# Two directions of an RWKV-7 scan: the chunk inverse multiplied onto the score rows outside the chain, 64-row score tiles, and a plain float32 output product

## The chip, the cores and the metric

The kernel runs on one core of one Trainium2 chip. The metric is the device time of one execution in microseconds (us), given as the median of several runs. PE is TensorE, DVE is VectorE, ACT is ScalarE, POOL is GpSimd, SP is SyncE, which here issues most of the DMAs.

## What is computed

One step of a two-layer trunk on 640 tokens (128 of a prompt, 512 of a sample) of 1024 features. Layer 0 mixes tokens with a spatial gate, layer 1 with RWKV-7, once forward and once backward in time; each is followed by an MLP. The change lies in layer 1. For each of 16 heads of 64 features a 64 x 64 state S is carried from token to token:

```python
def step(s, inp):
    r_t, w_t, k_t, v_t, kk_t, a_t = inp
    sa = jnp.einsum('bhij,bhj->bhi', s, -kk_t)
    s = (s * w_t[:, :, None, :]
         + sa[..., None] * (kk_t * a_t)[:, :, None, :]
         + v_t[..., None] * k_t[:, :, None, :])
    return s, jnp.einsum('bhij,bhj->bhi', s, r_t)
```

The outputs of the two directions are added, normalized per head, given a bonus term, multiplied by a gate, `g = sigmoid(xg @ g1) @ g2`, and go through `w_o` into the residual x.

## The kernel before

**Number format.** Most weight products split weights and activations into two parts of a fast format (float32r, "hi" and "lo") and add three products: hi hi, hi lo, lo hi. In the output product `mm3` does this. Other products are plain float32, which PE runs as two passes; each shows as two records in the trace.

**Tiles.** Features lie on partitions, 8 tiles of 128 features, two heads each (64 rows each). Tokens are cut into 10 chunks of 64 for each head, 2 of the prompt and 8 of the sample. q numbers pairs of chunks, e the chunk in a pair, ti one of the two feature tiles that are worked on together, d the direction, h the head in a tile. A group g is two feature tiles in one direction; there are 8 groups.

**Projections** (`rwkv_project`, lines 462 to 808). Tile t goes through the products for r, the low-rank decay and rate products (lines 624 to 626, PSUM tag z with two buffers), a quarter of the v products, and `finish` with `prep` for both directions (lines 629 to 669). `prep` makes running products of decays in Pt, then KR (k^ and r times decays, lines 651 and 653) and IT (the two kinds of state update rows, lines 660 to 665), and stores both to DRAM. KR, IT, Pt have one buffer each, tw two. For tiles 0 and 1 `score` (line 671) also makes the products IT^T k^ that a chunk's inverse takes and copies them to AT; the later tiles' come from the scans' fronts. The last tile's `finish` runs during the first scans.

**Inverse.** Within a chunk the tokens depend on each other; this is solved with a triangular 64 x 64 inverse for each chunk and head: 32 x 32 blocks by substitution on POOL and DVE (`inv_sub`), then two rounds of 32 x 32 products on PE (`merges`, gps and tps) that give TT, for a whole group at a time.

**Fronts** (`Front`, lines 884 to 933). A unit is one chunk pair of one feature tile, ten per group. `load` brings W (k^ and r rows of both heads with zeros in the other head's half, so that a 128-row product can serve both; the zeros are written to DRAM once, line 1608) and IT. `p1` multiplies them (p, line 910, two products of 256 columns), `ev` masks the scores into W and B and copies those that the inverse takes to AT, `tr` transposes IT (line 932) into B.

**The chain** (`part1`, `part2`). It runs through the chunks of a group. RZ holds, for each chunk, the state in one half of the partitions and v (later the solved rows) in the other. In a step, for each of the two feature tiles: za = W^T RZ (line 1026), a copy to zs on ACT (1029), za = TT^T zs (1039), two evacuations on ACT into RZ (1042). Meanwhile sy takes the state (1034, with an identity) and the r rows (1036); then come the products with B (1053, 1054), two evacuations on DVE with the decay factor into the next chunk's RZ (1060), and Y's (1063, 1065). The prompt's 2 chunks and the sample's 8 are independent, so that in a group's first four steps the two alternate.

**Order.** The code issues everything in program order, with hand-made tables that say at which of 20 positions of a group (two per step) a front's parts, the inverse, the merges, the adaLN products (`ada_core`) and the output product come. The chain's instructions have a higher priority, so a scheduler moves them ahead of others. Each engine then runs its own list in order.

**Output product** (`Tail`). `gate` multiplies y by the gate product; `early` does the first four feature tiles of w_o in groups 6 and 7, `end` the other four after the last step; weights and activations are split on ACT and on DVE or POOL (lines 1226 and 1227, 1192 and 1193).

## Time and profile before

| what | us |
|---|---|
| runs: median of 3 (lowest, highest) | 2092.6 (2089.22, 2100.25) |
| profiled execution: first to last instruction (span; the page gives no other time of it) | 2109.0 |
| PE busy in it | 1991.5 |
| DVE busy | 1162.9 |
| ACT busy | 774.5 |
| POOL busy | 389.3 |
| projections, last two thirds | 850 to 1072 |
| scans, from the first product with B to the last | 1107 to 1593 |
| after the scans, until layer 1's MLP | 1593 to 1636 |

The profile is one execution of its own, and its span is 16.4 us above the median of the runs. A row of the trace's groups reads: line, engine, operation, output tile from input tiles, form, count, then busy us and mean ns of one, then the idle time of the engine ahead of it and what ended it. A product's form "128*64" is rows by columns of the array that it takes; "128x64" is its moving operand. The record of a product spans its way through the array too, so the distance between two starts tells what one costs, and the sum of lengths does not. The granted clock is the share of full speed that TensorE's throttle passed.

### The profile page before, as it was taken

The numbers are of one execution on the slowest core, as the hardware profiler recorded it, in microseconds if no ns is written. First come the engines' busy times: TensorE is split into PE (matmuls) and PEld (weight loads), VectorE is DVE, ScalarE is ACT, GpSimd is POOL, SyncE is SP. The second block draws the span as 40 slices with busy tenths as digits, with TensorE's granted clock in tenths as the row PEclk, the third lists the DMA queues.
The fourth block names the chain that finished last, engine by engine and source line by source line (L and its number), as shares of the span: only waits on it lengthen the run. The fifth ranks groups of instructions, "written<-read, shape, count | busy, mean of one in ns | idle before, by whom it ended". The sixth has DMA issues, their size and how long they took to land.

```text
span 2109.0 us, 39157 instructions
## 1 busy us (share of the span) xinstructions
PE 1991.5 (94%) x15882; PEld 1739.6 (82%) x15882; DVE 1162.9 (55%) x2308; ACT 774.5 (37%) x1737; POOL 389.3 (18%) x689
## 2 busy tenths in 40 slices
PE   6999999999999789988869999999998999999997
PEld 5777889999999678877747766767787999999996
DVE  5435643333333796766786577787658533333334
ACT  5323531312222255444524444554434522222231
POOL 0000000000000200477551465465201000000000
PEclk9999999999999889987869879998799999999998
DMA  8777352222222033554655444552242222222221
GB/s 286 265 266 233 105 184 80 71 81 70 80 71 75 36 96 121 171 151 129 186 159 175 143 131 148 166 160 80 71 130 76 67 74 75 76 74 77 73 67 51
DMA packets 124438, 254.58 MB, mean 121 GB/s; under 512 B 24417, under 2 KB 63969, under 8 KB 124129
## 3 DMA queue, kind: packets, MB, share of 16 engines
q1 hardware_dynamic: 123824, 251.62, 37.3%
q8 instruction: 125, 2.05, 0.4%
q14 instruction: 57, 0.46, 0.1%
q10 hardware_dynamic: 432, 0.46, 0.1%
HBM read 214.67 MB, written 45.22 MB: 123 GB/s over the span
## 4 chain that ended last, share of the span: by engine, by line
PE 85%; DVE 6%; POOL 3%; ACT 2%; issue 2%; DMA 1%; SPq 0%; DVEq 0%; POOLq 0%; ACTq 0%
PE fmps L114 47%; PE zps L310 6%; PE p L910 4%; PE wops L1180 3%; PE vps L751 2%; PE za L1039 2%; PE za L1026 2%; PE sy L1053 2%; PE sy L1034 1%; PE rps L114 1%; PE trps L932 1%; PE adaps L1166 1%; PE adaps L122 1%; PE sy L1036 1%; PE tps L980 1%
## 5 line engine op out<-in xcount | busy, mean ns | idle before, releaser
L114 PE MATMUL fmps<-ahi,whi 128*128 128x256 f32 (+1 forms) x2272 | 534.6, 310 | 4.9 <-ACT ahi L100 3.1
L114 PE MATMUL fmps<-alo,whi 128*128 128x256 f32 (+1 forms) x2272 | 533.8, 309 | 1.3 <-DVE alo L101 1.3
L114 PE MATMUL fmps<-ahi,wlo 128*128 128x256 f32 (+1 forms) x2272 | 533.8, 309 | 0.0
L114 PEld LDWEIGHTS fmps<-ahi,whi 128*128 128x128 f32 x2272 | 414.4, 188 | 11.0 <-ACT ahi L100 6.3
L114 PEld LDWEIGHTS fmps<-alo,whi 128*128 128x128 f32 x2272 | 415.0, 188 | 2.1 <-DVE alo L101 1.8
L114 PEld LDWEIGHTS fmps<-ahi,wlo 128*128 128x128 f32 x2272 | 415.2, 188 | 1.0 <-issue 0.8
L88 ACT CAST whi<-wraw 128x1024 fp32r<-128x1024 f32 x174 | 182.6, 1050 | 632.6 <-PE fmps L114 538.2
L89 DVE TENSOR_TENSOR wlo<-wraw,whi 128x1024 fp32r<-128x1024 f32 x174 | 214.4, 1233 | 276.2 <-ACT whi L88 276.1
L283 DVE SCALAR_TENSOR_TENSOR x<-fmps,mod,x 128x128 f32<-128x128 f32 (+2 forms) x153 | 74.5, 527 | 305.4 <-PE fmps L114 305.4
L491 POOL TENSOR_TENSOR xx<-h 128x254 f32<-128x254 f32 (+1 forms) x16 | 12.1, 754 | 721.2 <-DVE h L210 706.1
L841 POOL TENSOR_TENSOR inv<-inv 128x220 f32<-128x220 f32 (+29 forms) x217 | 100.7, 464 | 114.4 <-DVE inv L834 57.7
L910 PE MATMUL p<-W,IT 128*128 128x256 f32 x320 | 109.6, 453 | 10.0 <-DVE B L925 5.9
L843 POOL TENSOR_TENSOR inv<-inv 128x220 f32<-128x220 f32 (+29 forms) x217 | 104.5, 482 | 16.9
L1042 ACT ACTIVATE RZ<-za 64x64 f32<-64x64 f32 x320 | 58.4, 214 | 66.7 <-PE za L1039 53.9
L1060 DVE TENSOR_TENSOR RZ<-sy,PC 64x64 f32<-64x64 f32 x256 | 49.4, 219 | 60.2 <-PE sy L1054 52.5
L101 DVE TENSOR_TENSOR alo<-rsq,ahi 128x640 fp32r<-128x640 f32 (+2 forms) x69 | 53.6, 776 | 45.6 <-ACT ahi L100 45.3
L100 ACT CAST ahi<-rsq 128x640 fp32r<-128x640 f32 (+2 forms) x69 | 47.5, 689 | 82.2 <-DVE rsq L435 81.8
L910 PEld LDWEIGHTS p<-W,IT 128*128 128x128 f32 x320 | 57.9, 211 | 22.9 <-DVE B L925 6.3
L1054 PE MATMUL sy<-RZ,B 128*64 128x64 f32 x640 | 72.6, 251 | 0.6 <-ACT RZ L1042 0.6
L1026 PEld LDWEIGHTS za<-RZ,W 128*64 128x64 f32 x640 | 43.5, 154 | 33.8 <-DVE RZ L1060 9.0
L1026 PE MATMUL za<-RZ,W 128*64 128x64 f32 x640 | 62.5, 254 | 8.4 <-DVE RZ L1080 5.9
L1036 PE MATMUL sy<-RZ,W 128*64 128x64 f32 x640 | 69.1, 249 | 0.0
(289 smaller groups left out, 3428.4 us busy)
## 6 DMA issues: line engine op xcount, KB each, us to landing
wraw<-w SPq DMA_DIRECT2D x126, 512.0 KB, 3.5
wraw<-ada SPq DMA_DIRECT2D x64, 512.0 KB, 4.9
W<-dKR SPq DMA_DIRECT2D x80, 256.0 KB, 3.5
adaw<-adac SPq DMA_DIRECT2D x32, 512.0 KB, 4.4
dKR<-zero SPq DMA_DIRECT2D x32, 320.0 KB, 6.3
dKR<-KR SPq DMA_DIRECT2D x32, 320.0 KB, 4.1
dIT<-IT SPq DMA_DIRECT2D x16, 640.0 KB, 3.3
IT<-dIT SPq DMA_DIRECT2D x80, 128.0 KB, 2.9
```

What stands on the lines that cost most here:

```text
L88: act.copy(hi[:, :n], r[:, :n])
L89: vec.tensor_tensor(out=lo[:, :n], in0=r[:, :n], in1=hi[:, :n], op=ALU.subtract)
L114: pe.matmul(ps[:, PS0 + t0:PS0 + t1], w, x[:, t0:t1], start=start, stop=stop)
L283: vec.scalar_tensor_tensor(out=X[n][:, t0:t1], in0=ps[:, t0 - r[0]:t1 - r[0]], scalar=mod[l][:, which, n, g:g + 1], in1=X[n][:, t0:t1], op ...
L310: pe.matmul(pss[i], x[:, i * P:(i + 1) * P], w[:, kq * 512:(kq + 1) * 512], start=(k == 0 and j == 0), stop=(k == KT - 1 and j == 2))
L841: eng.tensor_tensor(out=tv, in0=LA[:, s + 1:32, s:s + 1].to_broadcast([P, n, m]), in1=LX[:, s:s + 1, c0:c1].to_broadcast([P, n, m]), op=AL ...
L843: eng.tensor_tensor(out=LX[:, s + 1:32, c0:c1], in0=LX[:, s + 1:32, c0:c1], in1=tv, op=ALU.subtract)
L910: pe.matmul(ps[:, :, 2 * e:2 * e + 2].rearrange("p h s t -> p h (s t)"), IT[:, e], W[:, :, 2 * e:2 * e + 2].rearrange("p h s t -> p h (s t ...
L1026: pe.matmul(za[a0:a0 + 64, 0], W[:, h, 3 * e], RZ[:, ti, h, c], start=True, stop=True)
L1036: pe.matmul(sy[y0:y0 + 64, h], W[:, h, 1 + e], RZ[:, ti, h, c], start=h == 0, stop=False)
L1054: pe.matmul(sy[y0:y0 + 64, h], B[:, h, 3 * e], RZ[:, ti, h, c], start=False, stop=h == 1)
L1180: pe.matmul(ps, u, v, start=start and j == 0, stop=stop and j == 2)
```

## The change

1. **Chain.** New `wt` and `wp` make, per unit and before the chain gets there, WP: the k^ rows, an identity block and the masked scores, multiplied by the inverse TT. In the chain one product with WP (za) stands in place of two with a copy between. Its evacuation goes to ACT for one head and DVE for the other, and so does that of the next state. za has one PSUM buffer for both feature tiles instead of two.
2. **64-row tiles.** `load` brings T (k^ and IT, 128 rows, no zero halves) and the r rows into buffers whose other halves were zeroed once. `p1` makes eight products per unit on 64 rows, four with r and four with an identity (which replaces the transposes); the halves of the two heads go to different PSUM banks. p's PSUM tag has one buffer of two banks, shared with `wp`; `wt` has one bank, q. The 32 stores of zeros are gone.
3. **Scores in the projections.** `score` now runs for all tiles; from tile 2 on the result goes through tw to DRAM, and `load_AT` brings it back for a group.
4. **Output product.** Plain float32 instead of `mm3`: no splits, one product (two records) instead of three.
5. **Tables.** Merges come earlier in a group, fronts ahead of them are spread over the group, adaLN products start in group 2 instead of 3.

```diff
-                nc.sync.dma_start(out=dr["IT"][d, t], in_=IT.rearrange("p c s t -> p (c s t)"))
-                if t < 2:
-                    score(t, d, KR, IT)
+                nc.sync.dma_start(out=dr["T"][d, t, :, :, 2:6], in_=IT.rearrange("p (q e) s t -> p q (e s) t", e=2))
+                score(t, d, KR, IT, tw)
...
-                    u = U0[d] + 10 * t + 5 * b
-                    act.copy(ATs[d][:, u:u + 5], ps)
+                    if t < 2:
+                        u = U0[d] + 10 * t + 5 * b
+                        act.copy(ATs[d][:, u:u + 5], ps)
+                    else:
+                        act.copy(tw[:, 5 * b:5 * b + 5], ps)
+                if t >= 2:
+                    nc.sync.dma_start(out=dr["AT"][d, t], in_=tw)
...
-            cp = Pool(es, "cc", {"W": NL, "B": NL, "I": 5, "TT": 2})
+            cp = Pool(es, "cc", {"T": 6, "B": 8, "WT": 3, "WP": 8, "R": NR, "TT": 2, "b": 14})
...
-            pf = Pool(es, "cpf", {"p": 2, "m": 1}, PSUM)
+            pf = Pool(es, "cpf", {"p": 1, "q": 1, "m": 1}, PSUM)
...
+            Rs = [cp.tile([P, 2, 2, 64], F32, "R", f"R{j}") for j in range(NR)]
+            for R in Rs:
+                vec.memset(R, 0.0)
...
                 def p1(self, i):
                     u = self.buf[self.units[i]]
-                    W, B, IT, _ = u
-                    ps = pf.tile([P, 2, 4, 64], F32, "p", "p1")
+                    R, Tt = u[0], u[3]
+                    B = cp.tile([P, 2, 4, 64], F32, "B", "B")
+                    ps = pf.tile([P, 2, 8, 64], F32, "p", "p1")
                     for e in range(2):
-                        pe.matmul(ps[:, :, 2 * e:2 * e + 2].rearrange("p h s t -> p h (s t)"), IT[:, e],
-                                  W[:, :, 2 * e:2 * e + 2].rearrange("p h s t -> p h (s t)"), start=True, stop=True)
-                    u[3] = ps
+                        for h in range(2):
+                            a0 = 64 * h
+                            it = Tt[a0:a0 + 64, 2 + 2 * e:4 + 2 * e].rearrange("p s t -> p (s t)")
+                            pe.matmul(ps[:, h, 3 * e], it, R[a0:a0 + 64, h, e], start=True, stop=True)
+                        for h in range(2):
+                            a0 = 64 * h
+                            it = Tt[a0:a0 + 64, 2 + 2 * e:4 + 2 * e].rearrange("p s t -> p (s t)")
+                            pe.matmul(ps[:, h, 1 + e], it, ident[a0:a0 + 64, a0:a0 + 64], start=True, stop=True)
+                    vec.tensor_tensor(out=B[:, :, 0:4:3], in0=ps[:, :, 0:4:3], op=ALU.mult,
+                                      in1=masks[:, self.d, 1].unsqueeze(1).unsqueeze(1).to_broadcast([P, 2, 2, 64]))
+                    act.copy(B[:, :, 1:3], ps[:, :, 1:3])
+                    u[1] = B
...
+                def wt(self, i):
+                    u = self.buf[self.units[i]]
+                    Tt = u[3]
+                    ps = pf.tile([P, 2, 2, 64], F32, "q", "wtps")
+                    for e in range(2):
+                        for j in range(2):
+                            for h in range(2):
+                                a0 = 64 * h
+                                x = ident[a0:a0 + 64, a0:a0 + 64] if j == h else Tt[a0:a0 + 64, 3 - h + 2 * e]
+                                pe.matmul(ps[a0:a0 + 64, e, j], Tt[a0:a0 + 64, e], x, start=True, stop=True)
+                    W = cp.tile([P, 2, 2, 64], F32, "WT", "WT")
+                    vec.tensor_tensor(out=W, in0=ps, in1=mT[:, self.d].unsqueeze(1).to_broadcast([P, 2, 2, 64]), op=ALU.mult)
+                    u[3] = W
...
+                def wp(self, i):
                     ti, q = self.units[i]
...
+                    ps = pf.tile([P, 2, 8, 64], F32, "p", "wpps")
                     for e in range(2):
...
+                        for h in range(2):
+                            a0 = 64 * h
+                            pe.matmul(ps[:, h, e], W[a0:a0 + 64, e].rearrange("p s t -> p (s t)"),
+                                      TTs[self.d][a0:a0 + 64, 10 * ti + 2 * q + e], start=True, stop=True)
+                    WP = cp.tile([P, 2, 2, 64], F32, "WP", "WP")
+                    act.copy(WP, ps[:, :, 0:2])
+                    u[2] = WP
...
-                    za = pp.tile([P, 8, 64], F32, f"za{ti}", "za")[:, 0:2]
+                    R, _, WP, _ = fr.buf[ti, q]
+                    za = pp.tile([P, 8, 64], F32, "za", "za")[:, 0]
...
-                        pe.matmul(za[a0:a0 + 64, 0], W[:, h, 3 * e], RZ[:, ti, h, c], start=True, stop=True)
-                    zturn[0] = (zturn[0] + 1) % 4
-                    zs = L0[:, 1536 + 64 * zturn[0]:1600 + 64 * zturn[0]]
-                    act.copy(zs, za[:, 0])
+                        pe.matmul(za[a0:a0 + 64], WP[:, h, e], RZ[:, ti, h, c], start=True, stop=True)
...
-                        pe.matmul(za[a0:a0 + 64, 1], TT[a0:a0 + 64, 10 * ti + c], zs[a0:a0 + 64], start=True, stop=True)
-                    for h in range(2):
-                        a0 = 64 * h
-                        act.activation(out=RZ[a0:a0 + 64, ti, h, c], in_=za[a0:a0 + 64, 1], func=AF.Copy, scale=-1.0)
...
+                    act.activation(out=RZ[0:64, ti, 0, c], in_=za[0:64], func=AF.Copy, scale=-1.0)
+                    vec.tensor_scalar(out=RZ[64:128, ti, 1, c], in0=za[64:128], scalar1=-1.0, scalar2=None, op0=ALU.mult)
...
-                            vec.tensor_tensor(out=dst, in0=sy[s0:s0 + 64, h], in1=pc.to_broadcast([64, 64]), op=ALU.mult)
+                            if h:
+                                act.activation(out=dst, in_=sy[s0:s0 + 64, h], func=AF.Copy, scale=pc)
+                            else:
+                                vec.tensor_scalar(out=dst, in0=sy[s0:s0 + 64, h], scalar1=pc, scalar2=None, op0=ALU.mult)
...
-                            mm3(ps, self.w4[n][k - 4], self.ys[k][h], k == 4, k == 7)
+                            pe.matmul(ps, self.w4[n][k - 4], self.ys[k][h], start=k == 4, stop=k == 7)
...
-            MG = (11, 12, 15, 16, 17, 18, 19)
+            FA = (-8, -6, -4, -2, 0, 2, 4, 6, 8, 10)
+            MG = (4, 5, 7, 8, 9, 10, 11)
```

How the order moves, on PE. First a step of the fifth group, before: za and sy are the chain's first products, L1039 the inverse's, p (L910) and trps (L932) a later unit's front.

```order
L1026 MATMUL za<-RZ,W 64x64 x4
L1034 MATMUL sy<-RZ,cst 64x64 x2
L1036 MATMUL sy<-RZ,W 64x64 x2
L1034 MATMUL sy<-RZ,cst 64x64 x2
L1036 MATMUL sy<-RZ,W 64x64 x2
L1039 MATMUL za<-inv_7286,TT_9340 64x64 x4
L932 MATMUL trps<-cst,IT 128x2x64
L910 MATMUL p_13498<-W,IT 128x2x128 x2
L932 MATMUL trps<-cst,IT 128x2x64
L1053 MATMUL sy<-RZ,B 64x64 x2
```

The same step now: p at L927 (with r) and L931 (with an identity), gps (L1000) the merges' products, sy at L1069 and L1071.

```order
L1064 MATMUL za<-RZ,WP 64x64 x2
L1200 MATMUL adaps<-adaw,cs 32x256
L927 MATMUL p_14344<-R_9565,Tt 128x64 x2
L931 MATMUL p_14344<-cst,Tt 128x64 x2
L927 MATMUL p_14344<-R_9565,Tt 128x64 x2
L931 MATMUL p_14344<-cst,Tt 128x64 x2
L1000 MATMUL gps<-inv,AT 32x32 x3
L1069 MATMUL sy<-RZ,cst 64x64
L1000 MATMUL gps<-inv,AT 32x32
L1069 MATMUL sy<-RZ,cst 64x64
L1071 MATMUL sy<-RZ,R_9572 64x64
L1000 MATMUL gps<-inv,AT 32x32
```

The inverse's products are gone from the step, the two feature tiles' za stand apart, and pieces of other tile forms (64*128 for p, 32*32 for the merges) now stand among the chain's.

The second place is on PE too, in the projections: where a tile's bonus products (bops) and the next tile's norm (rbps) stand, before; vps are products of v, rps of r.

```order
L751 MATMUL vps<-wlo,ahi 128x256
L726 MATMUL bops<-rkh,k 128x2 x5
L114 MATMUL rbps<-rnT,AT 128x256
L114 MATMUL rbps<-rnT,AT 128x384
L114 MATMUL rps<-ahi,whi 128x256
L114 MATMUL rps<-ahi,whi 128x384
L114 MATMUL rps<-alo,whi 128x256
```

And now, at the same tile, with the second direction's scores (aps) four products of v later:

```order
L729 MATMUL bops<-rkh,k 128x2 x5
L114 MATMUL rbps<-rnT,AT 128x256
L114 MATMUL rbps<-rnT,AT 128x384
L754 MATMUL vps<-whi,ahi 128x256
L754 MATMUL vps<-whi,alo 128x256
L754 MATMUL vps<-whi,ahi 128x256
L754 MATMUL vps<-whi,alo 128x256
L677 MATMUL aps<-KR,IT 64x64 x20
L624 MATMUL zps<-hw,l2h 128x320
```

Twenty score products now stand between one tile's last v products and the next tile's decay products, and PE takes them in that order.

More of the change, by code (lines that the diff above doesn't have):

```diff
@@ L935, in inv_start, with load_AT @@
+            def load_AT(g):
+                p, d = divmod(g, 2)
+                for ti in range(2):
+                    u = U0[d] + 10 * ti
+                    nc.sync.dma_start(out=ATs[d][:, u:u + 10], in_=dr["AT"][d, 2 * p + ti])
             def inv_start(d):
@@ L1174, in ada_core, with bank, banks @@
                 gamma(1, 1)
-            def mm3(ps, w, x, start, stop):
-                for j, (u, v) in enumerate(((w[0], x[0]), (w[0], x[1]), (w[1], x[0]))):
-                    pe.matmul(ps, u, v, start=start and j == 0, stop=stop and j == 2)
-            def bank(n, tag="p"):
-                return (pf if tag in "pm" else pp).tile([P, 512], F32, tag, "wops")[:, 0:n]
+            def bank(n, tag="ada"):
+                return (pf if tag in "qm" else pp).tile([P, 512], F32, tag, "wops")[:, 0:n]
+            def banks(n):
+                t = pf.tile([P, 2, 512], F32, "p", "wops")
+                return [t[:, i, 0:n] for i in range(2)]
             def gated(n, ps, x, r):
@@ L1219, in tmp, with load @@
                     return t[:, 0:n]
-                def split(self, src, n, keep=None, eng=vec):
-                    r = self.tmp(n)
-                    nc.sync.dma_start(out=r, in_=src)
-                    hi, lo = (buf(c, [P, 512], F32R, "wos")[:, 0:n] for c in keep) if keep else \
-                        (self.tmp(n, "s"), self.tmp(n, "s"))
-                    act.copy(hi, r)
-                    eng.tensor_tensor(out=lo, in0=r, in1=hi, op=ALU.subtract)
-                    return [(hi[:, c:c + P], lo[:, c:c + P]) for c in range(0, n, P)]
+                def load(self, src, n, keep=None):
+                    r = buf(keep) if keep else self.tmp(n, "s")
+                    nc.sync.dma_start(out=r[:, 0:n], in_=src)
+                    return [r[:, c:c + P] for c in range(0, n, P)]
                 def gate(self, k):
@@ L1289, in late @@
                     nn.acc[1] = fw.tile([P, 384], F32, "acc", "acc1")
-                    self.ys += [full(*parts(fw)) for _ in range(2)]
-                    self.ys += [[one("W", LEN[0]), two("W", LEN[1])] for _ in range(2)]
+                    self.ys += [full(fw.tile([P, T], F32, "a", "ys")) for _ in range(4)]
                     self.fin = [self.finish(*q) for q in ((3, 5), (0, 1), (2, 3), (1, 2))]
@@ L1427, in rwkv_core @@
             pairs = [load_pair(0)]
-            for i in range(4):
-                front(fr[0], i)
             run(m)
@@ L1544, in rwkv_core @@
                 if g == 6:
+                    run(ada)
                     tail = Tail()
@@ L1678, in _pack @@
     d["adac"] = f(aw[1, :, :, 1:].transpose(2, 3, 0, 1, 5, 4, 6).reshape(2, 2, KT, P, 1024))
-    d["zero"] = np.zeros((64, 2 * T), np.float32)
     w = pt(i["sgu_w_in"][0])
```

207 lines of the change are left out of this document (76 added, 131 removed).

## The prediction

> **What bounds the kernel now.** I read the page's chain first: PE carries 85% of it, and most of that is products at line 114 that the change leaves alone. What it touches lies between 850 and 1636 us. There I cut the span into stages by where the scan's products begin and end. Columns: stretch, length, busy us of PE, PEld, DVE, ACT, POOL with instruction counts, granted clock, DMA share, GB/s.
>
> ```profile
> 850.00:1072.00 222.00, 194.57 (x1183) 164.97 (x1182) 151.87 (x131) 108.72 (x176) 137.90 (x172) 0.84 0.55 163
> 1072.00:1107.00 35.00, 20.46 (x216) 14.85 (x218) 31.36 (x65) 4.50 (x13) 21.35 (x42) 0.60 0.52 157
> 1107.00:1593.00 486.00, 477.50 (x5838) 349.81 (x5833) 346.97 (x1083) 226.90 (x888) 201.79 (x414) 0.89 0.44 133
> 1593.00:1636.00 43.00, 36.32 (x225) 32.61 (x225) 34.03 (x102) 19.53 (x47) 4.23 (x3) 0.95 0.21 68
> ```
>
> These are the last two thirds of the projections, the set-up of the scans, the scans, and the output product. In the scans PE looks 98% busy, but a product's record includes its pipeline latency, so that figure is no proof that PE is full. I therefore price PE's work by distances between starts. First the counts in the scan stage, grouped by form (records, then busy us and mean ns; a plain float32 product is two records):
>
> ```profile
> L910 PE MATMUL p<-W,IT 128*128 128x256 f32 x290 | 95.6, 437 | 0.0
> L1054 PE MATMUL sy<-RZ,B 128*64 128x64 f32 x640 | 72.6, 251 | 0.6 <-ACT RZ L1042 0.6
> ...
> L1034 PE MATMUL sy<-RZ,cst 128*64 128x64 f32 x568 | 58.1, 243 | 0.8 <-ACT Y L1063 0.7
> L1039 PE MATMUL za<-inv,TT 64*64 64x64 f32 x636 | 57.7, 250 | 1.5 <-ACT inv L1029 1.5
> L932 PE MATMUL trps<-cst,IT 128*128 128x128 f32 x152 | 38.4, 316 | 0.3 <-ACT B L933 0.3
> L1166 PE MATMUL adaps<-adaw,cs 128*32 128x256 f32 x256 | 32.8, 401 | 0.0
> L980 PE MATMUL tps<-inv 32*32 32x32 f32 x572 | 24.9, 229 | 0.1
> L962 PE MATMUL gps<-inv,AT 32*32 32x32 f32 x560 | 22.3, 228 | 2.1 <-ACT B L933 1.0 <-DVE inv L946 0.7 <-ACT TT L987 0.3
> ```
>
> The timeline gives the distances, at full clock (start, length, what):
>
> ```profile
> 859.10 1.38 PE L679 MATMUL aps<-KR,IT 64*64 64x64 f32 x40
> ...
> 866.03 1.17 PE L726 MATMUL bops<-rkh,k 128*128 128x2 f32 x10
> ...
> 1118.07 0.70 PE L910 MATMUL p<-W,IT 128*128 128x256 f32 x2
> ...
> 1122.19 1.13 PE L910 MATMUL p<-W,IT 128*128 128x256 f32 x4
> 1123.16 0.38 PE L932 MATMUL trps<-cst,IT 128*128 128x128 f32 x2
> ...
> 1396.80 0.22 PE L1036 MATMUL sy<-RZ,W 128*64 128x64 f32 x1
> ...
> 1396.85 0.22 PE L1036 MATMUL sy<-RZ,W 128*64 128x64 f32 x1
> ...
> 1396.91 0.22 PE L1036 MATMUL sy<-RZ,W 128*64 128x64 f32 x1
> 1397.06 0.46 PE L1039 MATMUL za<-inv,TT 64*64 64x64 f32 x8
> ...
> 1398.93 0.64 PE L1166 MATMUL adaps<-adaw,cs 128*32 128x256 f32 x8
> ```
>
> Each run of records ends with about 0.22 us of latency. What is left per record: p 0.216 us ((1.13 - 0.70) / 2); bops 0.106 ((1.17 - 0.22) / 9), which is the weight load alone, since it streams two columns; aps 0.030 ((1.38 - 0.22) / 39) on 64*64 tiles, where the two heads go side by side; ada 0.053; a transpose 0.11. The chain's 128*64 products start 0.057 apart on each of two column tiles, so 0.029 a record. And where the tile form changes (128*64 to 64*64) the next start comes after 0.15 instead of 0.057: 0.093 us for a change of form. From the chain of waits come the 32*32 products (1.24 / 40 = 0.031) and the output product (15.68 / 108 = 0.145):
>
> ```profile
> 1239.64 1.24 PE gps L962 x40
> ...
> 1554.85 15.68 PE wops L1180 x108
> ...
> 1592.69 0.63 ACT wos L1226
> ...
> 1593.38 1.52 POOL wos L1227
> 1594.92 2.52 DMA tmp<-wo
> ```
>
> So PE's work in the scans is: the five groups of 128*64 products, L1054 to L1034 in the rows, some 3,050 records x 0.029 = 88 us; p 63; transposes 17; L1039 19; ada 14; 32*32 35; some 226 output products 33; 60 transposes of y 7: 276. In the order of before I count 793 changes of form from the scans' first to last product: 74. Together 350. The stage offers 486 x 0.89 = 432 us of full clock, so PE waits some 82 us. It is near its own limit; the chain's latency accounts for the rest.
>
> **The change part by part. The chain.** A step loses the score copy, the inverse product, and half of two series of four evacuations, since ACT and DVE now take one head each:
>
> ```profile
> L1029 ACT COPY inv<-za 128x64 f32<-128x64 f32 x160 | 29.4, 213 | 63.9 <-PE za L1026 55.3 <-PE sy L1036 6.9
> ...
> 1397.56 0.68 ACT L1042 ACTIVATE RZ<-za 64x64 f32<-64x64 f32 x4 [0.69 <-PE za L1039]
> ...
> 1398.68 0.73 DVE L1060 TENSOR_TENSOR RZ<-sy,PC 64x64 f32<-64x64 f32 x4 [1.73 <-PE sy L1054]
> ```
>
> 0.21 (copy) + 0.22 (product) + two handovers of some 0.05 + 0.34 + 0.36 = 1.2 us a step, 98 us in 80 steps: more than the 82 that PE waits. The gain cannot exceed those waits.
>
> **Fronts.** Gone are 63 + 17 + 19 = 99 us of PE. In the new order, between the same two ends, stand 624 products of p (64*128), 608 of wt (64*64) and 316 of wp (64*128), two records each. wt goes as aps did: 1216 x 0.030 = 36. The others stream 64 columns under a 128-wide load, so the load sets them: 1880 x 0.106 = 200 us one after another, 100 if the two heads' row tiles run side by side. No row shows 64*128 pairs; aps, whose tiles differ in rows too, is the nearest, so I take 100. Net +37 (or +137).
>
> [...]
>
> **Changes of form.** The new order has 1298 in place of 793, because 64*128 and 64*64 pieces and single 32*32 products stand between the chain's: 505 x 0.093 = +47. Its bounds are 0 (every drain falls where PE waits anyway) and 47; I take 47, as PE is hardly idle.
>
> **Output product.** Three fast passes become two slow ones: for 256 columns 2 x 0.216 = 0.43 against 3 x 0.117 (0.145 x 256 / 320), for 384 0.65 against 0.52: +0.21 a pair. 38 pairs in the scans: +8.
>
> PE's work: 350 + 37 + 47 + 8 = 442 us, over the 432 that the stage has. Of the 82 us of waiting I leave 10. At the same clock: 452 / 0.89 = 508 us, **+22**. With no wait left it is 497 (+11), with all of them 589 (+103).
>
> **Projections.** Scores for all tiles: 12 more bursts of 1.38 us, minus the last tile's, which fall into the scans. Behind each stand its two copies on ACT, then a DMA in SP's queue (behind it the next stores and weight loads), and only then the tw buffer is free for the next tile's ACT op; KR stays held till the products have read it. Times at which a tile's r is evacuated:
>
> ```profile
> 859.74 0.68 ACT L686 COPY r<-rps 128x640 f32<-128x640 f32 x1
> 883.86 0.67 ACT L686 COPY r<-rps 128x640 f32<-128x640 f32 x1
> ...
> 951.99 0.67 ACT L686 COPY r<-rps 128x640 f32<-128x640 f32 x1
> 979.64 0.69 ACT L686 COPY r<-rps 128x640 f32<-128x640 f32 x1 [0.75 <-PE rps L114]
> ```
>
> With scores a tile took 24.1 us, without 27.7, so they can hide: 0. If each of the ten is exposed with one burst and as much again of clearing up, 28. I take **+8**, nearer the rows. Below nothing is excluded: work is only added.
>
> **Set-up**: 12 more memsets on DVE, six p, five wt and four wp instead of four fronts, one more product and copy before the first step, in 35 us of which PE uses 20 at clock 0.60: **+3** (-3 to +12). **Tail**: 32 pairs x 0.21 = +7 after the last step, but the splits on ACT and POOL and the wait for their tile's DMA (0.63 + 1.52 + 2.52 = 4.7, rows above) go: **+2** (-4 to +8). The DVE and ACT work of the other splits hides beside PE now; its going gives nothing. **Zeros**: 32 stores leave SP's queue; PE waited little for them: **-2** (-5 to 0).
>
> ```profile
> PEld adaps L122 <- DMA dKR<-zero: 1.5, 4, 0.4
> ```
>
> The fronts' loads fall in bytes (384 to 256 KB a unit) at a DMA share of 0.44: nothing. Sum: 22 + 8 + 3 + 2 - 2 = +33, made against the profiled execution, whose span is 2109.0 us, 16.4 above the median of the runs. I carry the difference to the median: 2092.6 + 33 = 2126.
>
> **The rivals.** *Faster: the drains lie in the waits.* DVE's evacuations at the end of steps:
>
> ```profile
> 1372.64 0.71 DVE L1060 TENSOR_TENSOR RZ<-sy,PC 64x64 f32<-64x64 f32 x4 [0.51 <-PE sy L1054]
> 1376.44 0.71 DVE L1060 TENSOR_TENSOR inv<-sy,PC 64x64 f32<-64x64 f32 x4 [0.22 <-PE sy L1054]
> ...
> 1386.03 0.73 DVE L1060 TENSOR_TENSOR RZ<-sy,PC 64x64 f32<-64x64 f32 x4 [0.55 <-PE sy L1054]
> 1392.36 0.77 DVE L1060 TENSOR_TENSOR RZ<-sy,PC 64x64 f32<-64x64 f32 x4 [0.17 <-PE sy L1054]
> ```
>
> In a group's first steps, where two chains are independent, a step takes 3.8 us; in the later ones, with one chain, 6.3. That speaks for the chain's latency. If drains cost nothing of their own, waiting is 156 us before; less 98 it is 58, and the stage takes (276 + 45 + 58) / 0.89 = 426: -60, in all 2044; halfway between this and my case is no change. It decides once more than half of the drains and nearly all of the 1.2 us count. Against it: the later steps also carry the merges, and starts on PE stand close together in them.
>
> *Slower by far: row tiles one after another.* (452 + 100) / 0.89 = 620: +134, in all 2238. Against it: aps.
>
> *The clock moves.* It was 0.89 with PE 98% busy. Short 64-row products in place of the 256-column p may lower it; at 0.80 the stage takes 565, +79, in all 2183. A denser PE may keep it at 1.0: 452, -34, in all 2070. [...]
>
> That the chain does not get shorter is excluded: the new order has one product between state and evacuation.
>
> **How the numbers follow.** My case has 0.45 (range 2100 to 2160), one after another 0.14, a lower clock 0.07, drains in the waits 0.27, a higher clock 0.07. About 0.5%, 10 us, is what a measurement can tell here. My case gives 0.40 slower and 0.05 same; drains 0.20 faster and 0.07 same; a higher clock 0.06 faster, 0.01 same; the other two slower. Faster 0.26, same 0.13, slower 0.61. Leaving out the outer half of the two extreme rivals, the range is 2045 to 2215.
>
> **What would show it.** Right: the scan stage near 508 us; in it 64*128 starts some 0.053 us a record, a change of form still 0.15; step ends evener, near 6 us; the projection stage within 10 us of 222. Wrong: steps under 5 us in the later half of a group; 64*128 records 0.106 apart; a granted clock far from 0.89 in the scans; r evacuations over 32 us apart.

## The result and the profile after

| | before | after |
|---|---|---|
| median of 4 runs, us (lowest, highest) | 2092.5 (2089.2, 2100.3) | 2488.2 (2486.0, 2491.4) |
| ratio, 95% interval | | 1.187 (1.183 to 1.192) |
| profiled execution, span | 2109.0 | 2484.6 |
| first product with B, last product with B | 1107.2, 1592.8 | 1083.7, 1956.0 |
| scans between the two | 485.6 | 872.4 |
| after them to the end | 516.2 | 528.6 |

The change made the kernel 18.7% slower; 1.6% was predicted. The spans differ by 375.6 us: 23.5 us less up to the first product with B, 386.8 more in the scans, 12.4 more behind them.

The same stages as in the prediction, cut where they now begin and end (stretch, length, busy us of PE, PEld, DVE, ACT, POOL with counts, granted clock, DMA share, GB/s): the projections, the set-up, the scans, the output product, and the rest.

```profile
850.00:1052.00 202.00, 190.89 (x1558) 162.77 (x1557) 138.06 (x123) 113.08 (x188) 138.98 (x162) 0.93 0.60 186
1052.00:1087.00 35.00, 24.52 (x347) 21.34 (x345) 30.47 (x66) 10.09 (x23) 23.16 (x40) 0.58 0.35 101
1087.00:1956.20 869.20, 866.24 (x7774) 656.57 (x7772) 357.86 (x1002) 202.89 (x640) 187.13 (x420) 0.56 0.24 72
1956.20:2012.00 55.80, 48.19 (x187) 30.51 (x186) 34.22 (x108) 16.39 (x39) 1.27 (x1) 1.00 0.13 46
2012.00:2484.00 472.00, 456.87 (x3092) 454.94 (x3092) 185.62 (x273) 130.39 (x186) 0.00 (x0) 0.98 0.23 71
```

The third row carries the whole result: the granted clock in the scans is 0.56, where before it was 0.89. DVE and ACT are busy for about as long as before (358 and 203 us, against 347 and 227) but now in nearly twice the time, so neither became the bound. The page's slices of 62 us, in tenths, show where it happens:

```profile
PE   7999999999979899989999999999999999999997
PEclk9999999999989999855555555565565999999998
```

PE stands at 9 all through the scans; from the slice at 1056 us to the end of the scans PEclk stands near 5. The products that the change brought are now the costliest groups of the scans (count, then busy us and mean ns of one):

```profile
L931 PE MATMUL p<-cst,Tt 64*128 64x64 f32 x616 | 123.6, 405 | 0.0
L927 PE MATMUL p<-R,Tt 64*128 64x64 f32 x616 | 119.8, 414 | 1.2 <-ACT WP L964 1.2
...
L947 PE MATMUL wtps<-cst,Tt 64*64 64x64 f32 x604 | 98.9, 313 | 0.0
L961 PE MATMUL wpps<-TT,WT 64*128 64x64 f32 x624 | 93.9, 412 | 0.9 <-ACT B L934 0.9
```

**How the clock moves.** The trace gives the granted clock as 1.0 or 0.5, and it changes at multiples of 3.41 us. Three such windows of after, around one change:

```profile
1327.60:1331.00 3.40, 3.40 (x64) 2.28 (x59) 1.93 (x7) 2.48 (x8) 0.00 (x0) 1.00 0.27 69
1331.00:1334.40 3.40, 3.40 (x36) 2.72 (x34) 1.55 (x7) 0.78 (x3) 0.00 (x0) 1.00 0.39 130
1334.40:1337.80 3.40, 3.40 (x43) 2.81 (x42) 1.71 (x7) 1.04 (x4) 0.00 (x0) 0.50 0.52 109
```

PE is busy for 3.40 of 3.40 us in each, and still the clock falls behind the second. A record's length includes its latency (in the prediction's rows sy records are 0.22 us long and start 0.05 to 0.06 apart), so the starts have to be looked at too: in the second window no two follow each other by more than 0.20 us. So no idle gap of anything like a window's length made it fall; there are only the short ones at each change of form, of 0.15 to 0.20 us from start to start. What stands in that window (timeline: start, length, what):

```profile
1331.00 0.33 PE L1084 MATMUL sy<-RZ,B 128*64 128x64 f32 x2
1331.26 0.43 PE L931 MATMUL p<-cst,Tt 64*128 64x64 f32 x2
1331.62 0.34 PE L1064 MATMUL za<-RZ,WP 128*64 128x64 f32 x4
1331.80 0.28 PE L1085 MATMUL sy<-RZ,B 128*64 128x64 f32 x2
1332.01 0.43 PE L931 MATMUL p<-cst,Tt 64*128 64x64 f32 x2
1332.37 0.33 PE L1084 MATMUL sy<-RZ,B 128*64 128x64 f32 x2
1332.62 0.43 PE L927 MATMUL p<-R,Tt 64*128 64x64 f32 x2
```

Every product takes half of the array and streams 64 columns, and the form changes after every two to six records. Compare a window of before that was at half clock and behind which the clock rose, at 1191.3 us:

```profile
1187.90:1191.30 3.40, 3.40 (x27) 2.45 (x26) 2.12 (x10) 0.89 (x3) 2.85 (x8) 0.50 0.56 178
1191.30:1194.70 3.40, 3.40 (x56) 2.62 (x52) 3.24 (x9) 1.87 (x9) 2.93 (x7) 1.00 0.68 204
...
1188.31 0.69 PE L932 MATMUL trps<-cst,IT 128*128 128x128 f32 x2
1188.79 1.91 PE L910 MATMUL p<-W,IT 128*128 128x256 f32 x4
1190.63 0.70 PE L1026 MATMUL za<-RZ,W 128*64 128x64 f32 x8
```

I count a window's *array work*: for each record, rows x columns of the array that it takes x columns streamed, with a p record of before (128 x 128 x 256, 0.216 us at full clock) as the unit; 16 of them would fill a full-clock window, and a float32r record counts half, as by the prediction's estimate from the output product's rows it takes 0.117 us for 256 columns. The window of before holds 4 such records of p, 2 transposes at 0.5, and 8 za records at 1/8, with some nine of sy at 1/8: 7.1 of 16, or 0.44. The window of after holds some 34 records at 1/8: 0.26. Counted so in the scans of all fourteen traces of this study (before, after, twelve experiments):

| array work of a window | at full clock: windows, next one at half | at half clock: windows, next one at full |
|---|---|---|
| under 0.25 | 105, 73 | 885, 18 |
| 0.25 to 0.30 | 113, 42 | 323, 26 |
| 0.30 to 0.34 | 121, 11 | 133, 25 |
| 0.34 to 0.38 | 149, 0 | 47, 33 |
| over 0.38 | 886, 0 | 36, 36 |

No window above 0.34 lost the clock, and few below it won it back. The bounds were read off these same windows, and a record that spans the edge of one can be shared out in other ways; counted where it starts, three of 1042 windows above 0.34 lost the clock, the highest at 0.35. Nothing like this shows when only streamed columns are counted: the windows of before and after behind which the clock fell hold from 0.38 to 0.78 by that count.

The measure is a fair account of the falls and a poorer one of the rises: half of them, 69 of 138, come from windows under 0.34. Many of those hold adaLN products, which take 128 rows but only 32 columns of the array. Of the windows under 0.34 at half clock, 31 of 142 with four or more such records rose, and 26 of 1093 with none. So the array's columns seem to count for less than their share. They do count for something: by rows x streamed columns alone, the clock fell behind windows of up to 0.75. No run here changes the array's columns by themselves, so their weight stays open.

The table also holds a trap. At half clock the same program did about half the work in a window, so what kept the clock up here did not bring it back. After's windows hold 0.46 on average at full clock and 0.21 at half, where only 1.4% are over 0.34; before's hold 0.51 and 0.28, where 16% are. Accordingly before loses the clock nine times in its scans and gets it back after 11 us on average; after loses it six times and stays low for 122 us on average, mostly until a run of adaLN or output products lifts it.

### The profile page after: what moved, and what is told of

Read it like the earlier page. It is cut to its first block, busy times and chain, and to the rows that moved or that the text cites. A ratio compares the mean times of both kernels' runs of the same rounds, so it can differ in the third digit from the quotient of the medians.

```text
span 2484.6 us, 43692 instructions
## 1 busy us (share of the span) xinstructions
PE 2390.1 (96%) x18294; PEld 2046.2 (82%) x18294; DVE 1159.3 (47%) x2229; ACT 758.5 (31%) x1505; POOL 376.0 (15%) x681
## 4 chain that ended last, share of the span: by engine, by line
PE 88%; POOL 4%; DVE 3%; ACT 2%; issue 2%; DMA 1%; SPq 0%; POOLq 0%; DVEq 0%; ACTq 0%
PE fmps L114 40%; PE zps L310 5%; PE wtps L947 4%; PE p L927 4%; PE wpps L961 3%; PE p L931 3%; PE sy L1084 3%; PE za L1064 3%; PE adaps L1200 2%; PE sy L1069 2%; PE wops L1279 2%; PE vps L754 2%; PE sy L1071 2%; PE sy L1085 2%; PE wops L1379 1%
## 5 line engine op out<-in xcount | busy, mean ns | idle before, releaser
L931 PE MATMUL p<-cst,Tt 64*128 64x64 f32 x640 | 128.1, 406 | 0.0
L927 PE MATMUL p<-R,Tt 64*128 64x64 f32 x640 | 124.7, 414 | 1.2 <-ACT WP L964 1.2
L1073 DVE TENSOR_SCALAR RZ<-za 64x64 f32<-64x64 f32 x160 | 36.4, 228 | 188.4 <-ACT RZ L1072 92.5
L1072 ACT ACTIVATE RZ<-za 64x64 f32<-64x64 f32 x160 | 34.7, 217 | 290.2 <-PE za L1064 149.5
L927 PEld LDWEIGHTS p<-R,Tt 64*128 64x128 f32 x640 | 94.7, 295 | 24.0 <-issue 6.0
L1085 PE MATMUL sy<-RZ,B 128*64 128x64 f32 x640 | 112.2, 311 | 0.3 <-ACT RZ L1072 0.2
L931 PEld LDWEIGHTS p<-cst,Tt 64*128 64x128 f32 x640 | 103.4, 304 | 7.7
L843 POOL TENSOR_TENSOR inv<-inv 128x220 f32<-128x220 f32 (+29 forms) x217 | 94.3, 435 | 96.4 <-DVE inv L836 57.4
L947 PE MATMUL wtps<-cst,Tt 64*64 64x64 f32 x640 | 103.9, 312 | 1.1 <-DVE WT L949 1.1
L1071 PE MATMUL sy<-RZ,R 128*64 128x64 f32 x640 | 104.6, 312 | 0.0
L1084 PE MATMUL sy<-RZ,B 128*64 128x64 f32 x576 | 103.3, 313 | 0.6 <-ACT RZ L1072 0.4
L845 POOL TENSOR_TENSOR inv<-inv 128x220 f32<-128x220 f32 (+29 forms) x217 | 98.1, 452 | 16.9
```

What stands on the lines that cost most here:

```text
L843: eng.tensor_tensor(out=tv, in0=LA[:, s + 1:32, s:s + 1].to_broadcast([P, n, m]), in1=LX[:, s:s + 1, c0:c1].to_broadcast([P, n, m]), op=AL ...
L845: eng.tensor_tensor(out=LX[:, s + 1:32, c0:c1], in0=LX[:, s + 1:32, c0:c1], in1=tv, op=ALU.subtract)
L927: pe.matmul(ps[:, h, 3 * e], it, R[a0:a0 + 64, h, e], start=True, stop=True)
L931: pe.matmul(ps[:, h, 1 + e], it, ident[a0:a0 + 64, a0:a0 + 64], start=True, stop=True)
L947: pe.matmul(ps[a0:a0 + 64, e, j], Tt[a0:a0 + 64, e], x, start=True, stop=True)
L1071: pe.matmul(sy[y0:y0 + 64, h], R[:, h, e], RZ[:, ti, h, c], start=h == 0, stop=False)
```

## The experiments

The edits are shown shortened. Theory A: the clock follows array work, and the 64-row products with 64 columns each let it fall; what it costs is the time at half clock. Rivals: another part of the change holds it down (B: the chain without its waits, the form changes, the tables), or TensorE is throttled because it no longer idles (C). For each run the row of its scans from the end of the first step to the end of the last is shown. It is of one execution, and small differences of its clock are not safe: before's trace has a granted clock of 0.937 over the whole execution, its other executions in this study mostly 0.934 to 0.951. Length x clock is the time that the scans would take at full clock, if all of it went with the clock; for before and after these rows are

```profile
1111.00:1593.00 482.00, 473.50 (x5798) 347.08 (x5794) 344.71 (x1075) 224.51 (x881) 198.49 (x405) 0.89 0.44 134
```

```profile
1091.00:1956.00 865.00, 862.04 (x7739) 653.33 (x7738) 355.23 (x994) 201.93 (x637) 183.68 (x413) 0.56 0.24 72
```

With the clock to three places (0.892, 0.563) that is 430 and 487 us of full clock.

**After, with p on all 128 rows.**

```diff
-    for h in range(2): pe.matmul(ps[:, h, 3 * e], it[a0:a0 + 64], R[a0:a0 + 64, h, e])
-    for h in range(2): pe.matmul(ps[:, h, 1 + e], it[a0:a0 + 64], ident[a0:a0 + 64, a0:a0 + 64])
+    pe.matmul(ps[:, :, 3 * e], it, R[:, :, e])
+    pe.matmul(ps[:, :, 1 + e], it, ident)
```

> The kernel after, with one edit: the score products and the transposes of p go over all 128 rows again (4 products of 128x128 weights and 128 columns for each pair of chunks instead of 8 on 64-row tiles); same results, nothing else changed. Theory A (the clock follows how much of the array the products use, and the 64-row tiles let it fall): the clock in the scans comes back from 0.53-0.55 to about 0.85-0.9 and the scans, 865 us, go to (442 + 45 us of dearer products + 10)/0.89 = about 560: 2180 us in all (2120 to 2260). Rival B (the clock falls for another part of the change: the chain without its waits, the form changes of the 64x64 and 64x128 products of wt and wp, the new tables): the clock stays below 0.6 and the dearer products come on top, 2490 to 2570 us.

```profile
1092.00:1763.00 671.00, 659.21 (x7132) 493.78 (x7128) 359.66 (x998) 201.16 (x638) 191.44 (x419) 0.80 0.31 93
```

2295.5 us, 1.091 of before (1.083 to 1.100), where after was 1.187. The products became dearer (534 us of full clock against 487, as expected) and the scans 194 us shorter, because the clock is 0.80. B falls as the main cause: chain, tables and wt, wp are as in after. (A run on before, below, shows that one part of B, the chain's evictions, lowers the clock too.) The clock is not quite back, so the time is above the expected 2180.

**After, with 160 unread wide products.**

```diff
+    for e in range(2):
+        pe.matmul(ps[:, e, 4:8], Tt[:, 2 + 2 * e:4 + 2 * e], R)     # 128 x 128, 256 columns
```

> The kernel after, with two products more for each pair of chunks, of 128x128 weights and 256 columns into unused places, read by nobody: the form of the p products of before, 160 in all, and nothing is taken away. Theory A (array use sets the clock): more work makes it faster; the clock in the scans rises to 0.85-0.9, scans (442 + 160 x 0.29 + 10)/0.89 = about 560 us instead of 865, 2185 us in all (2130 to 2280). Rival B (form changes, the chain or the tables hold the clock down): the products only add, 160 x 0.29/0.53 = 88 us, about 2575 us. Rival C (TensorE is throttled because it has no idle time left): the clock stays or falls further, 2575 us or more.

```profile
1106.00:1949.00 843.00, 835.35 (x8029) 620.46 (x8028) 363.89 (x981) 201.65 (x637) 183.45 (x395) 0.73 0.24 73
```

2480.0 us, 1.180 (1.174 to 1.187): hardly faster than after, with far more to do. The clock rose to 0.73, against B and C. But the 160 products cost 614 - 487 = 127 us of full clock, not the 46 that I had worked out. I took a record for a product; two records each make 69 us. Part of the rest is the wait at each change of form around them (0.15 us to the next start in before's rows), and part is not accounted for. The time is far from theory A's 2185.

**Before, with half the rows in the p products.**

```diff
-    pe.matmul(ps, IT[:, e], W[:, :, 2 * e:2 * e + 2])
+    pe.matmul(ps, IT[0:64, e], W[0:64, :, 2 * e:2 * e + 2])
```

> The kernel before, with one edit: the 285 p products of 256 columns take only 64 of their 128 rows (one head's share is left out of the sums, so the output is not the reference's). Same count, same columns, same order. Theory A in the reading that rows in use count: the clock in the scans falls from 0.89, to 0.7 or below, scans 482 us to over 570, 2180 us or more. Theory A in the reading that the columns streamed count, whatever the rows: clock 0.89, 2092 us within 15. Rival B (form changes, chain, tables): within 15 us of 2092 as well.

```profile
1105.00:1667.00 562.00, 554.35 (x5796) 386.52 (x5793) 343.47 (x1074) 226.76 (x881) 198.18 (x405) 0.75 0.38 115
```

2197.1 us, 1.049 (1.044 to 1.053). This is the cleanest run: the count of products, their columns, their order and all other engines' work are before's (one head's share is left out of the sums, so the values are not). Changes of form hardly rise, 823 recorded against 779. At full clock the scans would take 419 us, if anything less than 430. Only rows in use were taken away, and the clock went from 0.89 to 0.75 and the scans from 482 to 562 us. Here the rows counted, and the clock alone moved the time.

**Before, with the p products cut into four.**

```diff
-    pe.matmul(ps, IT[:, e], W[:, :, 2 * e:2 * e + 2])
+    for h in range(2):
+        for s in range(2):
+            pe.matmul(ps[:, h, 2 * e + s], IT[:, e], W[:, h, 2 * e + s])
```

> The kernel before, with one edit: each p product of 128 rows and 256 columns is cut into four of 64 columns with the same 128x128 weights (8 instead of 2 for each pair of chunks; same results). Rows in use stay, columns for each weight load go to a quarter. Theory A by rows: clock 0.89 as before, some 20 to 25 us of weight loads more, 2105 to 2125 us. Theory A by streaming (short products between weight loads let the clock fall): clock in the scans below 0.7, 2250 us or more. Rival B: 2105 to 2125 us.

```profile
1111.00:1785.00 674.00, 667.42 (x6677) 534.01 (x6677) 344.29 (x1076) 230.21 (x883) 192.90 (x393) 0.76 0.32 96
```

2302.8 us in the execution that the row is of, 2355.0 to 2393.0 in the other three: too uneven for an interval, but 10% over before at the least. The full array is used and the work is the same, but it takes 509 us of full clock instead of 430: the starts of these records lie 0.112 us apart at full clock (median), about what a weight load takes (0.106 in the prediction's rows), where a quarter of the 0.216 for 256 columns, 0.054, is my estimate for streaming 64. Spread over more time the same work falls under the bound more often: clock 0.76. This fits work per time, with short products lowering it as half rows do. By itself it does not set them apart from changes of form, which rise too, from 779 recorded to 1018.

**After, with the extra products spread evenly; with bursts; with both.** These three were to use the trap of the table: evenly spread work to hold the clock, bursts to lift it.

```diff
+    pe.matmul(zt[:, 4:8], ident, R)                        # at the head of part1: 160 times
```

> The kernel after with one unread product of 128x128 weights and 256 columns more at the head of every step of each tile (160, as many as in the run with extra products, where they stood two at a time; here they are spread evenly). They cost 160 x 2 x 0.213 = 68 us at full clock. Theory A2 (the clock goes by the array work of each single window of 3.4 us, and to rise from half takes more of it than to stay at full): spread evenly they bring a half-clock window only from 0.21-0.24 to about 0.25 of a full window's work, under the 0.34 from which rises were seen, so the clock stays low, 0.56 to 0.62, scans (487 + 68)/0.6 = 925 us, 2545 us in all. Rival (the clock goes by the mean of the array work, wherever it stands): as with the products two at a time, 2480 us.

```profile
1096.00:2086.00 990.00, 985.16 (x8082) 699.83 (x8079) 371.50 (x1001) 203.02 (x638) 187.61 (x414) 0.64 0.21 63
```

```diff
+    for i in range(10): pe.matmul(wb[:, i % 2, 4:8], ident, Rs[0])   # at the start of each chain
```

> The kernel after with ten such products in a row (8.5 us at half clock) at the start of each of the eight scans, nothing else: 8 x 10 x 0.427 = 34 us at full clock. Theory A2: each burst lifts the clock, which holds for a few windows and falls again; mean clock 0.65 to 0.7, scans (487 + 34)/0.68 = 766 us, 2390 us in all. Rival (mean of the array work): 0.60 to 0.62, 850 us, 2475 us.

```profile
1094.00:1960.00 866.00, 863.31 (x7904) 651.87 (x7904) 359.75 (x995) 202.13 (x638) 189.19 (x414) 0.64 0.24 72
```

> The kernel after with both: the even products and the eight bursts, 102 us of TensorE at full clock more than after. Theory A2: a burst lifts the clock and the even products (0.52 of the array at full clock, against 0.42 without them) hold it there: mean clock 0.9 or more, scans (487 + 102)/0.93 = 633 us, 2256 us in all, faster than after although 102 us of work were added. Rival (mean of the array work): clock about 0.78, scans 755 us, 2380 us. Rival (the clock has another cause): 2600 us or more.

```profile
1095.00:2047.00 952.00, 951.51 (x8242) 684.49 (x8242) 371.80 (x1000) 203.01 (x638) 187.81 (x411) 0.72 0.22 66
```

2601.9 us (1.241, 1.235 to 1.247), 2492.2 (1.193, 1.186 to 1.199), and 2574.6 (1.227, 1.219 to 1.235). One of the third's four executions took 6930.5 us at a granted clock of 1.0; there is no trace of it, and its cause is not known. The first agrees with the trap: the same number of products as in the second experiment, but spread evenly they give a clock of 0.64, not 0.73. The bursts lifted the clock (low stretches of 55 us instead of 122) and bought nothing; the time is nearer to the rival's 2475 than to the theory's 2390. My forecast for both together failed outright. In the run with even products each costs (634 - 487) / 160 = 0.92 us where I counted 0.43. The trace explains a part: as such a product stands between products of another form, the next start comes 0.63 us after its own at full clock (median of 56), and as late behind before's p products where one stands alone. The rest of the 0.92 is not accounted for. And windows full of p and sy pairs, or of the merges' products, still come, with 0.21 to 0.32 of array work, and drop the clock again. Extra work is no way to hold it up here.

**Before, with wide products among the 32x32 products of the merges.**

```diff
+    if c % 4 == 1: pe.matmul(wt[:, 10:14], ident, ident)     # 128 x 128, 128 columns, 96 in all
```

> The kernel before with three unread 128x128 products of 128 columns among the twenty 32x32 products of each merge step (96 in all, 20 us at full clock). In the trace of before ten of the twelve falls of the clock in the scans stand behind a window with 32x32 products. Theory A2: most of these falls go, clock 0.89 to 0.96, scans (429 + 20)/0.96 = 468 us against 482, 2078 us in all, the first version under both. Rival (the falls have another cause, as the chain's waits): clock 0.89 as before, 20/0.89 = 23 us more, 2115 us.

```profile
1115.00:1644.00 529.00, 523.85 (x5967) 378.20 (x5963) 349.84 (x1064) 224.40 (x879) 188.66 (x393) 0.89 0.39 121
```

2161.5 us, 1.031 (1.028 to 1.035). The theory's 2078 is missed, and the time is over the rival's 2115 as well. The clock in the two traces is the same 0.89; over whole executions it is 0.933 to 0.937, a little under before's median of 0.946 beside it. The products cost 39 us of full clock instead of 20. It fell ten times, where before's fell nine times (my twelve counted falls outside the scans), and mostly still behind windows with 32x32 products, at 0.18 to 0.32: three products were too few to fill them.

**Before, with the chain's evictions side by side: one part of the change alone.**

```diff
-    for h in range(2): act.activation(out=RZ[a0:a0 + 64, ti, h, c], in_=za[a0:a0 + 64, 1], scale=-1.0)
+    act.activation(out=RZ[0:64, ti, 0, c], in_=za[0:64, 1], scale=-1.0)
+    vec.tensor_scalar(out=RZ[64:128, ti, 1, c], in0=za[64:128, 1], scalar1=-1.0, op0=ALU.mult)
```

and the two state updates on VectorE and ScalarE, as in after.

> The kernel before with one part of the change alone: in the chain the two halves of RZ leave PSUM on ScalarE and VectorE side by side instead of one after another on ScalarE, and the two state updates on VectorE and ScalarE instead of both on VectorE. No product changes. Before's scans hold some 82 us of TensorE waits, most behind these. Theory: a fifth to a half of the waits goes, 15 to 40 us, the window's array work rises and the clock with it, a little (0.89 to 0.91): 2060 to 2080 us. Rival (other products fill the waits already, TensorE is the bound): 2092 us within 8. Rival (ScalarE is late with its longer queue): 2095 to 2110 us.

```profile
1113.00:1653.00 540.00, 530.03 (x5795) 377.60 (x5796) 358.64 (x1095) 241.82 (x867) 197.49 (x403) 0.80 0.39 119
```

2162.2 us, 1.033 (1.029 to 1.037): slower than every forecast. At full clock the scans would take 432 us, as before: TensorE's products did fill the waits already. The loss is the clock's, 0.80: the low stretches are 35 us long instead of 11, and at half clock 6% of windows are over 0.34 instead of 16% (4 and 5 windows). Whole executions agree with the traces here: their clock is 0.906 to 0.923, before's beside it 0.934 to 0.951. The order now mixes the wide products more finely among the chain's (897 changes of form recorded, 779 before).

**After, with p as wide as before's.**

```diff
+    # R holds r (even), the identity, r (odd): 384 columns
+    pe.matmul(ps[:, 4 * e:4 * e + 4], it, R[:, 2 * e:2 * e + 4])      # 2 products of 256 columns
```

> The kernel after with the p products as wide as before's: 128 rows, 256 columns (two heads of r and the identity in one operand), 2 for each pair of chunks instead of 8 on 64-row tiles; two rings of the output product are a tile or two shorter. Against the run with p on 128 rows and 128 columns the same array work in fewer products and fewer form changes. Theory (array work in each window sets the clock): clock 0.80 to 0.88, TensorE's cycles 534 less some 15, scans 520/0.84 = 620 us, 2240 us in all (2200 to 2290); still over before, since its products take 520 us at full clock against 430. Rival (what brought 2295 was the 64x128 form gone, and width is nothing): 2295 us within 15.

```profile
1097.00:1713.00 616.00, 607.26 (x6826) 435.56 (x6826) 363.94 (x1081) 209.09 (x713) 195.35 (x418) 0.83 0.33 99
```

2252.1 us, 1.072 (1.065 to 1.079), 12 us over the forecast. (To make room, two buffers of the output product are shortened as well.) Of the 396 us that the change lost, these two products for each pair of chunks bring back 236. The rest is mostly that the scans take 508 us of full clock.

**Bunched p products, on before and on the run with the chain's evictions.**

```diff
+    with tc.high_priority(200):                              # in p1 and around tr's transposes
-    TRS = (3, 4, 6, 6, 7, 8, 9, 10, 11, 13)
+    TRS = (1, 2, 3, 4, 5, 6, 7, 8, 9, 10)
```

> The kernel before with the same products in another order: the p products and the transposes of B go ahead of everything else that is ready, so that they stand four to eight together (P P P P, T T P P T T P P) and not one or two between the chain's. Theory A2 (a window at half clock must hold 0.34 of a full window's array work to lift the clock, so wide products bunched together lift it sooner): low stretches shorter than 11 us on average, clock 0.90 to 0.94, scans 455 to 475 us, 2065 to 2085 us in all. Rival (order is nothing to the clock, and the bunches stand in the chain's way): clock 0.89, 2095 to 2120 us.

```profile
1107.00:1585.00 478.00, 451.94 (x5785) 338.06 (x5785) 360.00 (x1065) 223.78 (x876) 186.25 (x399) 0.93 0.44 133
```

> The run with the chain's evictions side by side (2162 us, clock 0.80 in the scans, low stretches of 35 us on average) with the same bunching of the p products and transposes. Theory A2: its low stretches fall to some 15 us, the clock comes back to 0.87 to 0.9, scans 432/0.885 = 488 us, 2110 us in all; with the chain's gain perhaps 2080. Rival (the finer mixing of products had nothing to do with the clock): 2150 to 2175 us.

```profile
1108.00:1641.00 533.00, 505.16 (x5786) 369.06 (x5785) 371.93 (x1088) 239.89 (x866) 190.42 (x406) 0.85 0.40 119
```

2103.3 us, 1.0045 (1.0027 to 1.0063), and 2165.1, 1.035 (1.033 to 1.038). In the traces the clock did what theory A2 says: 0.93 instead of 0.89, 0.85 instead of 0.80, low stretches of 6 us instead of 11, and 15 instead of 35. But the executions without a trace hardly bear it out. Over whole executions the clock is 0.941 to 0.950 with the bunches and 0.940 to 0.948 for before beside it; on the run with the chain's evictions 0.915 to 0.930, its trace the highest of six, against 0.906 to 0.923. So a gain from bunching is suggested at most. The times are in the rivals' ranges, 2095 to 2120 and 2150 to 2175. With the bunches PE stands idle for 26 of 478 us, where before had 8.5 of 482, and the scans take 445 us of full clock instead of 430, and 455 instead of 432. No version here beats before. Whether the fine mixing cost the run with the chain's evictions its clock stays open.

As a forecast, theory A did less well than as an account. Its times held for three runs (half rows, narrow products, wide products) and missed in the rest, by the clock as well as by what the edits cost TensorE at full clock.

## Why the prediction was wrong, step by step

**The step that failed** is "At the same clock: 452 / 0.89 = 508 us, +22". By length x clock the scans from first to last product with B hold 485.6 x 0.89 = 432 us of full clock before and 872.4 x 0.56 = 489 after. At 0.89 that would be 549 us, +63; the other 324 of the 387 us are the fall from 0.89 to 0.56. The half-rows run shows such a fall by itself, and the two runs with p on 128 rows undo much of it on after's side.

**The rival was there and mis-sized.** "The clock moves" named short 64-row products in place of the 256-column p; I gave it 0.07 and a clock of 0.80, with no row from which to take how far. I read 0.89 as a level that might shift a little. It is a mean of 1.0 and 0.5, and the trace of before had the material: what stands in a window ahead of each change, and how long the clock stays low. The sign by which I said I would see an error, a granted clock far from 0.89 in the scans, is the one that came.

**Its other half**, a denser PE that keeps the clock at 1.0, had no row behind it either. PE did get denser, busy for 866.24 of 869.20 us where before it was for 477.50 of 486.00, and the clock fell. The rows at 1331 show a fall with PE busy for 3.40 of 3.40 us and no two starts more than 0.20 us apart.

**The work of TensorE.** I predicted 452 us at full clock and 487 to 489 was run. Row tiles do go side by side:

```profile
1560.76 1.12 PE L961 MATMUL wpps<-TT,WT 64*128 64x64 f32 x8
...
1569.47 0.47 PE L927 MATMUL p<-R,Tt 64*128 64x64 f32 x1
```

Eight records in four pairs, at half clock: (1.12 - 0.47) / 3 = 0.217 us a pair, which makes 0.054 a record at full clock, as I had taken (0.053). So "one after another" falls, and the 100 us that I took from aps hold. The count of form changes was right too (1287 recorded, 1298 counted), and so was its price at full clock: the next start still comes after 0.15 us. At half clock, where after mostly ran, it comes 0.244 us later instead of 0.107, which makes 0.069 us of full clock against my 0.093. What was wrong was the 82 us of waits before, of which I let 72 go. I had priced the chain's 128*64 records at 0.029 us, the best case, while the mean distance to a next one of the same form is 0.038 in sy in both traces and 0.040 to 0.044 in za. For some 3,020 records that is about 30 us that I took for waits and that could not go. By itself that is most of the missing 36, but the cheaper changes of form at half clock save about as much again, so the sum does not close.

**The rival "drains lie in the waits"** falls. The groups above leave PE idle for 1.2 us at most, and nothing was gained: TensorE's work was the bound, as the run with the chain's evictions shows on before as well.

**Projections and set-up** were to cost 8 + 3 us and gave 23.5 back. The last r is evacuated at 1030.6 instead of 1043.0, and from there to the first product with B it takes 53.1 us instead of 64.2. From one tile's r to the next it takes 27.8 to 31.6 us where scores came in, 27.7 to 37.7 before, so they hide, as the nearer row said. TensorE's time at full clock in the projections is the same, 222 x 0.84 = 186 and 202 x 0.93 = 188 us, with the clock higher; that more score products raise it would fit the table, but no run changed them alone.

**Tail**: +2 predicted, +12.8 measured (43 us to the MLP before, 55.8 now, at clock 1.00). The +7 for two slow passes in place of three fast ones may stand; the 5 that I set against it for the splits did not come, so they were probably beside the products all along. Some 6 us more are not accounted for. No run tried the output product alone.

**The others.** With no single rival's time near 2488, a range from my own cases could not hold it: its upper end was half of "one after another", which is another mechanism.

## What to carry to other kernels

In these traces a granted clock between 0.5 and 1 was a mean over time of these two, so before pricing a change on TensorE look at which windows lose the clock, which get it back, and how much of the array each keeps working. Here swapping wide 128-row products for 64-row, 64-column ones took the scans' clock from 0.89 to 0.56: +63 us at the old clock became +387, so such a swap must be priced at the new one. Busy TensorE was no protection (3.40 of 3.40 us ahead of the fall at 1334.4): what went with the clock was rows x columns x streamed columns per time (the weight of the columns is open), and once the clock was down the same program had only about half of that to offer (after's windows 0.21 on average, at full clock 0.46). Work added to hold the clock cost more than its own time (160 products two at a time 127 us of full clock where I count 69, spread evenly 147), and brought no more than it cost: at best 2480.0 us against 2488.2.

## What the runs showed of the hardware

- In the scans of the fourteen traces the clock is 1.0 or 0.5 and changes at multiples of 3.41 us. By the counts above it fell only behind windows under about 0.35 of the array's work, and at half clock it rose behind all 36 over 0.38; between 0.34 and 0.38 it rose 33 times in 47. In after it rose five times behind windows with less, 0.14 to 0.30, four of them with products on 128 rows and 32 columns, the fifth (at 1112.5 us) with 64*64 and 128*64 products alone.
- Behind a 128x128 product of 256 columns the next start came after 0.63 us at full clock when it stood alone between products of other forms (median of 56 in the run with even products, and before), against 0.43 in a row of its kind.
- Cutting 256-column products into four of 64 columns with the same weights cost 509 - 430 = 79 us at full clock for some 145 products, half a microsecond each, changes of form included.
